# Two pads of 32 bytes ahead of the split activation tiles of a hybrid decoder block on one core

## The chip, the core and the metric

One core of one Trainium2 chip runs the whole program; the other seven are not used. The metric is the device time of one execution in microseconds (us), shown as the median of several runs. The engines are TensorE (PE for its matmuls, PEld for its weight loads), VectorE (DVE), ScalarE (ACT), GpSimd (POOL) and the queue of SyncE (SP), which issues the weight transfers.

## What is computed

The reference is one decoder block on 256 tokens of width 2048, in float32: a normed input projected to 14092 columns, four branches beside each other (a gated linear recurrence, a forgetting attention, a state space branch, an RWKV-7 branch), each gated and projected back, an output projection, a feed-forward part with a short convolution, and a gated addition at the end.

```python
def reference(x, p, ...):
    xn = rmsnorm(h, mix_norm[i])
    proj = jnp.einsum('bsd,dn->bsn', xn, w_in[i])
    ...
    gates = jax.nn.sigmoid(g_raw.astype(jnp.float32)).reshape(Bsz, S, N_BRANCH, D)
    for j in range(1, N_BRANCH):
        merged = merged + gates[:, :, j] * jnp.einsum('bsc,cd->bsd', branches[j], w_branch[i, j])
    h = h + jnp.einsum('bsd,de->bse', merged, w_out[i]).astype(h.dtype)
    hn = rmsnorm(h, ffn_norm[i])
    u = causal_dwconv(jnp.einsum('bsd,df->bsf', hn, w_up[i]), ffn_conv_w[i], ffn_conv_b[i])
    u_gate, u_val = jnp.split(u, 2, axis=-1)
    h = h + jnp.einsum('bsf,fd->bsd', jax.nn.gelu(u_gate) * u_val, w_down[i]).astype(h.dtype)
    pg = jax.nn.sigmoid(jnp.einsum('bsd,de->bse', rmsnorm(h, ple_norm[i]), w_ple_gate[i]))
    h = h + (pg * jnp.einsum('bsq,qd->bsd', p[i], w_ple[i])).astype(h.dtype)
    return h
```

## The kernel before

Every large product is made of weights that are streamed once from memory and activations that stay in SBUF, feature by token (128 features of a tile on the partitions, 256 tokens along each). Both are split into a high and a low part that the TensorE multiplies as float32r, so that one product becomes three: high by high, high by low, low by high.

**Weights.** `chunk` (lines 199 to 202) loads 512 KB into a tile `wr` (four buffers). `split` (204 to 210) lets ScalarE copy it to the high part `wh` (L208) and VectorE subtract that for the low part `wl` (L209), three buffers of 4096 bytes a partition each. A chunk holds four contraction steps k by two column blocks m.

**Activations.** `split_x` (226 to 230) puts the high part into the first 1024 bytes of a tile and the low part into the next 1024. Such tiles are `x` (pool `xp`, 16 buffers), `f` (the 44 tiles of the feed-forward part, pool `fp`), `p`, and for the output projection eight tiles `d` (pool `dp`) and eight quarters of tiles `e` (pool `bc`). `split_act` (220 to 224) makes two separate tiles instead, from pool `bp`, which the trace calls `sb`; the ys of the branches are of this kind.

**Products.** `product` (235 to 245) does one step of wide products in two matmuls: `wl` as stationary with the 256 columns of the high part, `wh` as stationary with all 512 columns of the tile. I call the two a pair; the wl matmul comes first except at k = 0. Where the activations come as two halves (the gates, from `xg`, line 1099, and the branch projections), lines 287 to 289 do three matmuls of 256 columns, with `wh`, `wh` and `wl`.

**Order.** `gemm_fm` (252 to 298) is one unit: for each chunk of four k it goes over m and k, then evacuates the PSUM banks. The units follow in program order: `w_ax`, 19 units of projections and `w_v` with the branches interleaved by `pump`, up to about 310 us; then gates (`gate_unit`, 1101) and branch projections (`branch_unit`, 1109) up to 840 us; `w_out` to 935; `w_up` (44 units, all with `x` tiles) to 1427; `w_down` (8 units of 44 k, with `f` tiles) to 1675; `w_ple_gate` (with `x`) to the end. The two priorities `g` and `m` and the order that the framework's list scheduler makes of them are the same in both kernels.

**Where tiles lie.** Pools are laid out in the order in which they are opened: `cst`, `wp`, `xp`, `sp`, then `bc`, `bp`, `dp`, and after these are closed `pp` and `fp` in their place. Tiles start at multiples of 32 bytes. In the built programs the start of a partition's bytes stands like this to 64:

| tile | what it is | first address before | beyond a multiple of 64, before | after |
|---|---|---|---|---|
| wh, wl | split weights, stationary | 36608, 48896 | 0 | 0 |
| x | split activations | 61184 | 0 | 32 |
| s | temporaries of 1024 bytes | 93952 | 0 | 32 |
| e | half of the activations of w_out | 119552 | 0 | 32 |
| p, f | split activations behind the branches | 119552, 123648 | 0 | 32 |
| sb | split ys of the branches, other temporaries | 175776 | 32 | 32 |
| d | the other half of the activations of w_out | 212640 | 32 | 32 |

Within a tile all the offsets that a wide matmul uses are multiples of 512 bytes, so the column holds for every matmul of the tile.

Of the kernel before, what the change touches and what calls it, by code (L numbers as in the profile page):

```python
# [7 lines left out]
F32 = mybir.dt.float32  # L8
# [6 lines left out]
P = 128  # L15
# [70 lines left out]
def body(tc, T, out, dbg=None):  # L86
    nc = tc.nc
    V, A, G, PE = nc.vector, nc.scalar, nc.gpsimd, nc.tensor
    ctx = ExitStack()
# [66 lines left out]

    cst = ctx.enter_context(tc.tile_pool(name="cst", bufs=1))
    wp = ctx.enter_context(tc.tile_pool(name="wp", bufs=2))
    xp = ctx.enter_context(tc.tile_pool(name="xp", bufs=16))
    sp = ctx.enter_context(tc.tile_pool(name="sp", bufs=25))  # L160
    psG = ctx.enter_context(tc.tile_pool(name="psG", bufs=4, space=bass.MemoryType.PSUM))
# [12 lines left out]
    bc_ = bctx.enter_context(tc.tile_pool(name="bc", bufs=1))  # L174
# [187 lines left out]
    act(junk, junk, AF.Identity)  # L362
    xraw, xs = [], []
    warm = bc_.tile([P, 512], F32, name="e", tag="e", bufs=3)
    V.memset(warm, 0.0)
    for k in range(KD // 2):
        xraw.append(dslot())
# [954 lines left out]
```

## Time and profile before

| | us |
|---|---|
| median of 3 runs (1774.45, 1783.17, 1775.72) | 1775.72 |
| the profiled execution's own time | 1783.29 |
| its span, first to last instruction | 1781.4 |
| TensorE busy in it | 1761.6 (99%) |
| VectorE, ScalarE, GpSimd busy | 1239.1, 942.8, 103.2 |

A busy share of TensorE close to 100% says only that matmuls overlap one another: the shown duration of one (some 390 ns for 512 columns) is longer than the time from one start to the next. What a matmul costs in a full stream is therefore read as a stretch of time divided by the matmuls that start in it. In the views by stretches the number behind x counts every instruction that lies in the stretch, so a stretch cut at the start of one matmul and of another counts one to three more than start in it.

### The profile page before, as it was taken

The page shows a single profiled execution, that of the slowest core. Times are in us where ns is not written, and L with a number is a line of the kernel's source. Part 1 is how long each engine was busy: PE and PEld are TensorE (multiplying, and loading weights), DVE is VectorE, ACT ScalarE, POOL GpSimd, SP SyncE. Part 2 cuts the span into 40 slices and gives each one's busy share as a digit, 9 for nine tenths or more (in the row PEclk, how much of TensorE's full clock was granted, in tenths as well). Part 3 has the DMA queues.
Part 4 walks back from the last instruction along what each step waited for, and adds up shares of the span by engine and source line. Part 5 has one row for each costly group of instructions (what it writes and reads, how often), then busy time and mean ns, then how long its engine had stood idle before and what let it go on. Part 6 is the DMA issues. An engine that isn't in the chain of part 4 may idle for free.

```text
span 1781.4 us, 29735 instructions
## 1 busy us (share of the span) xinstructions
PE 1761.6 (99%) x11621; PEld 1586.7 (89%) x11621; DVE 1239.1 (70%) x1998; ACT 942.8 (53%) x1422; POOL 103.2 (6%) x160
## 2 busy tenths in 40 slices
PE   8999999999999999999999999999999999999998
PEld 7887888999999999999888888888888888888887
DVE  8778667687789623567777777777777765555666
ACT  7577445556644423545556555555555544444554
POOL 4000000002310100000110000000000000000000
PEclk9999999999999979999999999999999999999999
DMA  8556556556665733555775555555556666665574
GB/s 278 172 169 193 166 171 211 185 173 204 204 211 177 246 107 113 171 179 180 232 229 188 188 188 184 186 187 189 186 184 195 210 204 191 191 190 185 171 227 131
DMA packets 98844, 336.27 MB, mean 189 GB/s; under 512 B 12330, under 2 KB 16592, under 8 KB 98704
## 3 DMA queue, kind: packets, MB, share of 16 engines
q1 hardware_dynamic: 90528, 310.94, 54.8%
q0 software_dynamic: 7456, 21.81, 4.2%
q8 instruction: 91, 1.49, 0.4%
q10 hardware_dynamic: 720, 1.63, 0.3%
q14 instruction: 49, 0.40, 0.1%
HBM read 324.85 MB, written 9.48 MB: 188 GB/s over the span
## 4 chain that ended last, share of the span: by engine, by line
PE 72%; issue 8%; DMA 1%; DVE 1%; POOL 0%; ACT 0%; POOLq 0%; DVEq 0%
PE pg L132 70%; PE pb L135 1%; PE pb L132 1%; DMA e<-fox_rn 0%; DVE wl L209 0%; DMA d<-rw_gn 0%; DMA rw_q<-e 0%; DMA rw_gn<-sb 0%; DVE s L100 0%; DVE e L888 0%; DVE sb L120 0%; POOL qbd L903 0%; POOL e L927 0%; DVE e L100 0%; POOL qat L899 0%
## 5 line engine op out<-in xcount | busy, mean ns | idle before, releaser
L132 PE MATMUL pg<-x,wh 128*128 128x512 f32 (+1 forms) x4384 | 1194.6, 346 | 2.4 <-DVE sb L100 2.4
L209 DVE TENSOR_TENSOR wl<-wr,wh 128x1024 fp32r<-128x1024 f32 (+1 forms) x592 | 717.3, 1213 | 433.1 <-ACT wh L208 425.3
L208 ACT CAST wh<-wr 128x1024 fp32r<-128x1024 f32 (+1 forms) x592 | 615.4, 1040 | 664.1 <-PE pg L132 519.7
L132 PE MATMUL pg<-x,wl 128*128 128x256 f32 (+1 forms) x3344 | 923.5, 284 | 10.1 <-DVE wl L209 10.1
L132 PEld LDWEIGHTS pg<-x,wh 128*128 128x128 f32 x4384 | 757.1, 190 | 100.8 <-issue 2.6
L132 PEld LDWEIGHTS pg<-x,wl 128*128 128x128 f32 (+1 forms) x3344 | 635.0, 190 | 24.9 <-DVE wl L209 12.9
L132 PE MATMUL pg<-f,wh 128*128 128x512 f32 x704 | 244.9, 395 | 0.0
L132 PE MATMUL pg<-f,wl 128*128 128x256 f32 x704 | 194.3, 280 | 0.0
L132 PEld LDWEIGHTS pg<-f,wh 128*128 128x128 f32 x704 | 131.6, 188 | 29.8
L132 PEld LDWEIGHTS pg<-f,wl 128*128 128x128 f32 x704 | 132.8, 189 | 1.1
L132 PE MATMUL pg<-sb,wh 128*128 128x256 f32 x512 | 95.5, 286 | 0.0
L120 DVE SCALAR_TENSOR_TENSOR s<-s,prm 128x255 f32<-128x255 f32 (+1 forms) x176 | 84.2, 478 | 1.7 <-ACT s L127 1.0
L132 PEld LDWEIGHTS pg<-sb,wh 128*128 128x128 f32 x512 | 80.6, 193 | 0.4
L249 ACT COPY s<-pg 128x256 f32<-128x256 f32 x136 | 49.6, 366 | 46.7 <-PE pg L132 46.2
L132 PE MATMUL pg<-sb,wl 128*128 128x256 f32 x256 | 73.2, 287 | 0.0
L100 DVE TENSOR_TENSOR s<-s 128x256 f32<-128x256 f32 (+1 forms) x172 | 70.7, 420 | 1.4
L100 DVE TENSOR_TENSOR s<-s,pg 128x256 f32<-128x256 f32 x136 | 56.3, 415 | 10.0 <-ACT s L249 8.3
L127 ACT ACTIVATE s<-s 128x256 f32<-128x256 f32 x140 | 56.4, 411 | 13.0 <-DVE s L100 12.7
L127 ACT ACTIVATE s<-s,prm 128x256 f32<-128x256 f32 x88 | 52.4, 595 | 0.7 <-DVE s L100 0.7
L127 ACT ACT_TABLE_LOAD x39 | 50.0, 1283 | 1.8 <-PEq L1312 1.2
L132 PEld LDWEIGHTS pg<-sb,wl 128*128 128x128 f32 x256 | 49.1, 192 | 0.5 <-issue 0.3
L132 PE MATMUL pg<-e,wh 128*128 128x512 f32 x128 | 45.6, 399 | 0.0
(232 smaller groups left out, 1211.2 us busy)
## 6 DMA issues: line engine op xcount, KB each, us to landing
wr<-in_w_up_dram SPq DMA_DIRECT2D x176, 512.0 KB, 3.6
wr<-in_w_g_dram SPq DMA_DIRECT2D x128, 512.0 KB, 3.7
wr<-in_w_down_dram SPq DMA_DIRECT2D x88, 512.0 KB, 4.2
wr<-in_w_p_dram SPq DMA_DIRECT2D x76, 512.0 KB, 3.9
wr<-in_w_branch_dram SPq DMA_DIRECT2D x32, 512.0 KB, 3.6
wr<-in_w_out_dram SPq DMA_DIRECT2D x32, 512.0 KB, 4.3
wr<-in_w_ple_gate_dram SPq DMA_DIRECT2D x32, 512.0 KB, 4.5
wr<-in_w_v_dram SPq DMA_DIRECT2D x8, 512.0 KB, 4.1
```

Source lines behind the costliest of these rows:

```text
L100: V.tensor_tensor(o, a, b, op=op)
L120: V.scalar_tensor_tensor(o, a, s, b, op0=op0, op1=op1)
L127: A.activation(o, i, f, **kw)
L132: return f(*a, **kw)
L135: f(*a, **kw)
L208: A.copy(wh, wr)
L209: V.tensor_tensor(wl, wr, wh.bitcast(F32), op=ALU.subtract)
L249: A.copy(o, pt[:, S:])
```

## The change

Before the pools `xp` and `sp` a pool with one tile of 32 bytes a partition is opened, so that all tiles behind it start 32 bytes later. In pool `bc`, behind the three `e` buffers, another tile of 32 bytes is allotted, so that the tiles behind it (the constants, `sb`, `d`) start 64 bytes later than before. Nothing reads or writes the pads. The lists of instructions of all engines, with their waits, sizes and buffers in turn, are the same in both kernels; only addresses differ: `x`, `s`, `e`, `p` and `f` by 32, what lies behind the second pad by 64, and `wr`, `wh`, `wl`, `prm2` and `R` by nothing.

```diff
     wp = ctx.enter_context(tc.tile_pool(name="wp", bufs=2))
+
+
+    pad = ctx.enter_context(tc.tile_pool(name="pad", bufs=1))
+    pad.tile([P, 8], F32, name="pad0")
     xp = ctx.enter_context(tc.tile_pool(name="xp", bufs=16))
...
     warm = bc_.tile([P, 512], F32, name="e", tag="e", bufs=3)
+    bc_.tile([P, 8], F32, name="pad1")
     V.memset(warm, 0.0)
```

## Rows read from the trace of the kernel before

**Rows 1.** The page's first part (busy us, share of the span, instructions of each engine), and the engines' shares of the chain of work that ended last.

```profile
PE 1761.6 (99%) x11621; PEld 1586.7 (89%) x11621; DVE 1239.1 (70%) x1998; ACT 942.8 (53%) x1422; POOL 103.2 (6%) x160
...
PE 72%; issue 8%; DMA 1%; DVE 1%; POOL 0%; ACT 0%; POOLq 0%; DVEq 0%
```

**Rows 2.** Who waited for whom over the whole span: engine, what it was to write, its line, whom it waited for; us in total, times, the longest.

```profile
ACT wh L208 <- PE pg L132: 519.7, 338, 4.2
...
DVE wl L209 <- ACT wh L208: 425.3, 352, 8.4
...
PE pg L132 <- DVE wl L209: 10.1, 7, 3.8
```

**Rows 3.** Stretches, TensorE alone: from and to, length, busy us and count, granted clock, share and rate of the DMA engines. The first is 360 gate matmuls on x, the second 160 of branch projections on sb, the third 400 pairs of w_up on x, the last three 80 pairs each of w_down on f, in its first, second and third unit.

```profile
770.11:813.31 43.20, 43.20 (x363) 1.00 0.60 190
820.59:839.36 18.77, 18.77 (x162) 1.00 0.55 179
1000.12:1141.29 141.17, 141.17 (x803) 1.00 0.59 187
1430.68:1458.94 28.26, 28.26 (x162) 1.00 0.66 205
1461.05:1488.78 27.73, 27.73 (x162) 1.00 0.63 196
1492.03:1519.76 27.73, 27.73 (x163) 1.00 0.62 191
```

**Rows 4.** Stretches in w_out, all engines: length, busy us and count of PE, PEld, DVE, ACT and POOL, granted clock, DMA share and rate. Each is eight pairs: the first and third on tiles d, the second and fourth on tiles e.

```profile
844.03:846.81 2.78, 2.78 (x17) 2.45 (x16) 2.78 (x6) 1.68 (x3) 0.00 (x0) 1.00 0.52 164
846.81:849.63 2.82, 2.82 (x17) 2.45 (x16) 2.12 (x4) 1.36 (x2) 0.00 (x0) 1.00 0.75 241
900.06:902.83 2.77, 2.77 (x17) 2.44 (x16) 2.60 (x6) 1.21 (x2) 0.61 (x2) 1.00 0.82 220
902.83:905.65 2.82, 2.82 (x17) 2.45 (x16) 1.22 (x1) 1.05 (x1) 0.00 (x0) 1.00 0.86 311
```

**Rows 5.** Groups of TensorE's matmuls by form in stretches 0 to 310 (first row), 310 to 600 (next two), 600 to 740 (two), 740 to 840 (two), 840 to 935, 935 to 1427, 1427 to 1675 and 1675 to the end (one each): count, then busy us and mean ns of one as modelled.

```profile
L132 PE MATMUL pg<-x,wh 128*128 128x512 f32 x640 | 226.0, 399 | 2.4 <-DVE sb L100 2.4
...
L132 PE MATMUL pg<-x,wh 128*128 128x256 f32 x1201 | 220.7, 284 | 0.0
L132 PE MATMUL pg<-x,wl 128*128 128x256 f32 x601 | 170.5, 286 | 0.0
...
L132 PE MATMUL pg<-x,wh 128*128 128x256 f32 x384 | 76.9, 296 | 0.0
L132 PE MATMUL pg<-x,wl 128*128 128x256 f32 x192 | 56.7, 295 | 0.0
...
L132 PE MATMUL pg<-x,wh 128*128 128x256 f32 x418 | 76.6, 287 | 0.0
L132 PE MATMUL pg<-x,wl 128*128 128x256 f32 x209 | 59.5, 286 | 1.9 <-DVE wl L209 1.9
...
L132 PE MATMUL pg<-e,wh 128*128 128x512 f32 x128 | 45.6, 399 | 0.0
...
L132 PE MATMUL pg<-x,wh 128*128 128x512 f32 x1395 | 486.3, 398 | 0.0
...
L132 PE MATMUL pg<-f,wh 128*128 128x512 f32 x704 | 244.9, 395 | 0.0
...
L132 PE MATMUL pg<-x,wh 128*128 128x512 f32 x253 | 89.5, 398 | 0.0
```

**Rows 6.** Stretches, all engines, columns as in rows 4: the gates and branch projections until 600, w_up, w_down.

```profile
310.00:600.00 290.00, 290.00 (x2406) 288.73 (x2405) 233.21 (x401) 156.95 (x235) 41.38 (x62) 1.00 0.63 196
...
935.00:1427.00 492.00, 492.00 (x2792) 427.51 (x2791) 374.29 (x610) 283.00 (x437) 5.92 (x11) 1.00 0.60 190
1427.00:1675.00 248.00, 248.00 (x1421) 216.85 (x1420) 134.74 (x162) 110.54 (x141) 3.76 (x7) 1.00 0.61 191
```

**Rows 7.** Groups of VectorE and ScalarE instructions by form: the same elementwise operation on tiles s and on tiles sb, and the copy to a high part on f and on sb (count, busy us, mean ns).

```profile
L100 DVE TENSOR_TENSOR s<-s 128x256 f32<-128x256 f32 x170 | 69.8, 420 | 1.4
...
L100 DVE TENSOR_TENSOR sb<-sb 128x256 f32<-128x256 f32 x34 | 13.9, 421 | 5.1 <-ACT sb L127 4.8
...
L214 ACT CAST f<-s 128x256 fp32r<-128x256 f32 x44 | 17.4, 394 | 0.0
...
L214 ACT CAST sb<-sb 128x256 fp32r<-128x256 f32 x38 | 14.7, 403 | 15.4 <-DVE sb L100 11.9 <-DVE sb L120 3.1
```

**Rows 8.** Stretches of ten us about the narrow matmuls of the RWKV branch, columns as in rows 4; the granted clock is the third number from the end.

```profile
620.00:630.00 10.00, 10.00 (x108) 9.71 (x106) 1.65 (x2) 2.81 (x5) 0.00 (x0) 0.73 0.21 71
630.00:640.00 10.00, 10.00 (x51) 8.12 (x49) 2.50 (x4) 2.54 (x6) 0.00 (x0) 0.50 0.16 54
640.00:650.00 10.00, 10.00 (x66) 9.18 (x67) 2.10 (x4) 2.81 (x4) 0.00 (x0) 0.58 0.17 52
...
760.00:770.00 10.00, 10.00 (x73) 10.00 (x73) 10.00 (x21) 5.36 (x10) 0.00 (x0) 0.83 0.62 177
```

**Rows 9.** The timeline of TensorE inside w_up: start in us, duration in us, engine, line, operation, output and operands.

```profile
1103.63 0.40 PE L132 MATMUL pg<-x,wh 128*128 128x512 f32 x1
1103.87 0.28 PE L132 MATMUL pg<-x,wl 128*128 128x256 f32 x1
1103.99 0.40 PE L132 MATMUL pg<-x,wh 128*128 128x512 f32 x1
```

## The prediction

> **What bounds the kernel now.** I read the shares first, then the waits, then the pitch of the matmuls. TensorE is busy 99% of the span, and 72% of the chain that ended last is its own work [rows 1]. The waits say the same from the other side: the longest total is ScalarE waiting 519.7 us for TensorE to give back a buffer `wh`, VectorE waits 425.3 us behind ScalarE, while TensorE waited for VectorE's low parts 10.1 us in all [rows 2]. So the weights are ready ahead of time nearly everywhere, and time goes from one matmul's start to the next. What the change can touch is this pitch, and only where a stretch holds matmuls back to back.
>
> The pitch is not the same everywhere. In w_up, on tiles `x`, 400 pairs took 141.17 us, 352.9 ns a pair. In w_down, on tiles `f`, 80 pairs took 28.26 us in the first unit (353.3 ns a pair) and 27.73 us in the second and third (346.6) [rows 3]. All at full granted clock, with the DMA engines at about the same load. In w_out one and the same unit goes over tiles `d` and then over tiles `e`, with the same weights buffers, sizes and order: eight pairs on `d` took 2.78 and 2.77 us (346.9 ns a pair), eight on `e` 2.82 twice (352.5) [rows 4]. With 256 columns throughout, 360 gate matmuls on `x` took 43.20 us, 120.0 ns each, and 160 of a branch projection on `sb` 18.77 us, 117.3 ns each [rows 3].
>
> Set beside the table of addresses, `d` and `sb` start 32 bytes beyond a multiple of 64 and are quick, `x` and `e` start on one and are slow, `f` starts on one and is either. That is an experiment that the kernel already holds: the change puts `x`, `e`, `f` and `p` where `d` and `sb` stand. `f` tells something more. Its two speeds go by whole units at unchanged addresses, so an offset of 0 does not force the slow pitch; it allows a slow rhythm that a unit falls into at its start and stays in. In no stretch on `d` or `sb` that I looked at does that rhythm appear.
>
> **The change part by part.** No instruction is added, removed or moved, and no wait. The pads cost no time. What may change is (a) the matmul pitch, (b) the time that other engines need for tiles at other addresses, (c) phases against the clock.
>
> (a) *Wide pairs.* The quick price is that of `d`, 346.9; the slow one 352.5 (e) to 352.9 (x, with the starts of units in it). I take 5.7 ns a pair, between the 5.6 of `e` against `d` and the 6.0 of `x` against `d`. The counts are in [rows 5]:
> w_up, 1395 pairs: 8.0 us. Half of w_out, 128 pairs on `e`: 0.7. The last stage, 253 pairs on `x`: 1.4, and 0.1 for the 32 on `p`. w_down: 248.0 us hold 1421 matmuls [rows 6], 13 more than the 704 pairs on `f`; less these 2.3 us it is 349.0 ns a pair, 2.1 above `d`: 1.5. The projections before 310 us, 640 pairs: here weights come late at times and units are mixed with narrow matmuls; from nothing (all already quick or hidden by other waits) to 3.6 us (640 by 5.7); I take the middle, 2.0, because no row gives it.
>
> *Matmuls of 256 columns.* On `x` there are 1201, 601, 384, 192, 418 and 209, in all 3005 [rows 5]. At 120.0 less 117.3 ns they give 8.1 us. Not all run at 120.0: about 100 lie where the clock is halved [rows 8], and those behind a change from `sb` may start quick. I take 7.0; the lower bound is about half, 4, should the branch's own work on VectorE, busy 233 of 290 us from 310 to 600 [rows 6], pace this stage in part. Against this stands that TensorE had no idle time there at all, 290.00 busy of 290.00, and only 1.9 us behind `wl` later [rows 5, 6].
>
> Sum: 8.0 + 0.7 + 1.4 + 0.1 + 1.5 + 2.0 + 7.0 = 20.7 us. What covers for the faster TensorE: it must be fed 1.6 to 2.3% sooner. In w_up VectorE is busy 374 of 492 us and the DMA engines 60% [rows 6], so nobody comes near to taking the bound over. ScalarE's wait for a buffer gets shorter by what TensorE gains, and becomes the reserve that is used up: 519.7 us of it against 20.7.
>
> (b) *Other engines.* The same elementwise operation takes VectorE 420 ns on `s` and 421 on `sb`, and ScalarE's copy to a high part 394 on `f` and 403 on `sb` [rows 7]. With `s` moved to the offset of `sb` I cost this at nothing; even 9 ns on all of ScalarE's copies would lie under its waits. The upper bound is some 1 us, at the ends of units, where an evacuation is awaited.
>
> (c) *Clock.* Around 620 to 650 us, behind a run of narrow matmuls of the RWKV branch, the granted clock is 0.73, 0.50 and 0.58 in three stretches of ten us, and 0.83 once more at 760 [rows 8]. At half clock the time is twice that at full: 2.7 + 5.0 + 4.2 + 1.7 = 13.6 us are lost there. TensorE will come there earlier, by perhaps 5 us, and how long the clock stays at 1.2 GHz can come out otherwise, by all of this downward and by about as much upward. I take no change.
>
> The profiled execution took 1783.29 us, so the sum for it is 1762.6. The median of the runs shown is 7.6 us below it, and one of the three runs, 1783.17, lies where the profiled one does. The saving is a sum over matmuls that every run makes, so I take it off the median: 1775.7 less 20.7 is **1755.0 us**.
>
> **The rivals.**
>
> *The offset does nothing.* `d` and `sb` also lie highest in SBUF, and the two rhythms of `f` show that starts of units matter. If the starts decide alone, w_up may stay as it is and units of `f` may change sides: the mean of 349.0 between 346.6 and 353.3 makes five in eight quick, and these to slow would cost 440 by 6.7 ns, 2.9 us. The result is 1774 to 1779. Against it: tiles `f` spread over the same addresses as `sb` and are slow in whole units; and the turn from `d` to `e` comes inside a unit, twice alike [rows 4]. This is also what the Trainium skill would have: "TensorE: Matmul & The Clock Gate", section "Step-by-step: what each phase is for", says that the array has two separate read ports to SBUF, so that loading the next weights takes nothing from the matmul that runs. By it, where the two operands lie to each other could not matter, and the time would stay at 1775.7. The trace does not agree as it stands: 2.78 against 2.82 us for the same eight pairs. Chance 0.12.
>
> *It locks in a worse place (slower).* `d` and `sb` stand 160 bytes beyond a multiple of 256, `x` and `f` will stand 32 beyond one. If a longer period than 64 bytes counts, the new place may hold a rhythm slower than 352.9 ns; from there on it is a loss. Within the slow rhythm single pairs are longer than its mean: from one wide matmul's start to the next 0.36 us [rows 9], some 361 ns. If all wide pairs took that: 8.1 ns by about 1776 pairs on `x` and `e` of w_up, w_out and the last stage are 14.4 us, 12.0 by 704 on `f` 8.4: 1798.5. Nothing in the trace shows a stretch at that mean. Chance 0.04.
>
> *It works in part.* The wide pairs follow `d`, the gates don't follow `sb`, since `sb` holds its two halves in separate tiles and `xg` in one: 13.7 us, 1762. The other way round, 9 us: 1766.7. Chance 0.16, most of it still faster by over 0.5%.
>
> **How the numbers follow.** The forecast has 0.68, the partial case 0.16, no effect 0.12, the worse rhythm 0.04. Changes under 0.5% (8.9 us) are about what a measurement of this kernel can't tell from none, so the mark for faster is 1766.8. Faster: 0.68 and 0.13 of the partial case, 0.81; same: 0.12 and 0.03, 0.15; slower 0.04. The range goes down to 1746: the lowest run, 1774.45, less the upper ends of the terms (1395 by 6.0 is 8.4, then 0.8, 1.5, 0.1, 1.6, 3.6, 8.1; 24.1 in all) is 1750, and a part of the clock's 13.6 us below that. It goes up to 1770: the partial case at 1766.7 and a part of the clock's loss. That leaves out no effect and the worse rhythm.
>
> **What would show it.** Right: w_up from its first to its last unit in about 484 us in place of 492; 80 pairs of w_down near 27.75 us in every unit, none at 28.26; `e` like `d` in w_out; gate matmuls at 117.3 ns; TensorE's waits as small as before. Wrong: w_up still at 352.9 ns a pair (no effect), or over it (a worse rhythm); gates at 120.0 (partial); pitches as forecast, but waits for `wl` of more than 5 us above the 10.1 (someone else becomes the bound); or all this right and the stretches at half clock longer by 15 us or more.

## The result and the profile after

The changed kernel takes 1755.67 us, the median of 4 runs (1752.78 to 1759.45); the kernel before, beside it, 1776.98 (1774.45 to 1783.17). The ratio is 0.9884, with a 95% interval of 0.9856 to 0.9913. Timed a second time, six runs against eleven, the ratio was 0.9907 (0.9877 to 0.9937). The profiled execution took 1754.74 us, with a span of 1752.9.

The same instructions as in [rows 3], now in the changed kernel (from and to, length, busy us and count, granted clock, DMA share and rate): 360 gate matmuls on x, 160 of a branch projection on sb, 400 pairs of w_up, 80 pairs each of w_down's first three units.

```profile
753.85:795.85 42.00, 42.00 (x363) 1.00 0.62 202
802.98:821.91 18.93, 18.93 (x162) 1.00 0.57 181
981.31:1120.23 138.92, 138.92 (x803) 1.00 0.60 190
1405.02:1432.75 27.73, 27.73 (x162) 1.00 0.68 211
1434.84:1462.58 27.74, 27.74 (x161) 1.00 0.62 198
1465.84:1493.57 27.73, 27.73 (x162) 1.00 0.61 190
```

The gates went from 120.0 to 116.7 ns a matmul, w_up from 352.9 to 347.3 ns a pair, and w_down's slow unit is gone: all three shown take 27.73 or 27.74 us. The matmuls on sb, which the second pad moved by 64 bytes, became slower, from 117.3 to 118.3 ns. The eight pairs on d and e of [rows 4], same view:

```profile
826.61:829.44 2.83, 2.83 (x18) 1.00 0.53 122
829.44:832.22 2.78, 2.78 (x18) 1.00 0.76 237
882.36:885.14 2.78, 2.78 (x18) 1.00 0.71 200
885.14:887.92 2.78, 2.78 (x17) 1.00 0.91 332
```

The tiles e (second and fourth row) fell from 2.82 to 2.78 us. The tiles d, also moved by 64, are slow in one stretch (2.83 for 2.78) and as quick as before in the other (2.78 for 2.77). The whole of w_up, against the row of [rows 6], all engines (PE, PEld, DVE, ACT, POOL):

```profile
919.90:1404.00 484.10, 484.10 (x2790) 427.67 (x2789) 374.52 (x610) 283.17 (x438) 5.92 (x11) 1.00 0.61 193
```

484.10 us in place of 492.00, with VectorE and ScalarE busy for as long as before: nobody else became the bound. The waits of TensorE for low parts are 10.5 us in all against 10.1, but they are longer in the projections (first 312 us). In the changed kernel:

```profile
PE pg L132 <- DVE wl L213: 10.0, 7, 3.8
```

and in the kernel before:

```profile
PE pg L132 <- DVE wl L209: 8.2, 6, 3.8
```

Of the 1.8 us more, 1.2 lie in the first 20 us, where e1 (below), with the pitches of the kernel before, waits as long. The first 20 us of the kernel before, of the changed one and of e1:

```profile
PE pg L132 <- DVE wl L209: 0.7, 2, 0.4
...
PE pg L132 <- DVE wl L213: 1.9, 2, 1.4
...
PE pg L132 <- DVE wl L211: 1.8, 2, 1.5
```

One difference can't be put down to the change, as its repeat below shows. The stretches about the narrow matmuls, as in [rows 8], in the profiled execution of the changed kernel.

```profile
620.00:630.00 10.00, 10.00 (x124) 9.08 (x123) 3.64 (x6) 3.90 (x8) 0.00 (x0) 1.00 0.20 57
630.00:640.00 10.00, 10.00 (x97) 9.04 (x98) 3.71 (x5) 3.23 (x5) 0.00 (x0) 1.00 0.32 104
640.00:650.00 10.00, 10.00 (x119) 9.80 (x118) 3.21 (x5) 2.59 (x4) 0.75 (x1) 1.00 0.62 210
```

The granted clock is 1.00 here, where it was 0.73, 0.50 and 0.58. So the two profiled executions differ by 28.6 us, of which about 12 are the clock's: the mean over the span is 0.997 against 0.990. To compare kernels apart from it I take from each run's time its span times one less its mean clock, and call this *less the clock*. It is an estimate. It is somewhat too large, since it takes the lower clock for half the speed, and gate matmuls at 0.50 took 213.4 ns and not twice their 120.0 (rows in the last section); and the clocks are recorded to 0.001, which leaves 0.9 us either way in each run.

### The profile page after: what moved, and what is told of

Read it like the earlier page. It is cut to its first block, busy times and chain, and to the rows that moved or that the text cites. A ratio compares the mean times of both kernels' runs of the same rounds, so it can differ in the third digit from the quotient of the medians.

```text
span 1752.9 us, 29735 instructions
## 1 busy us (share of the span) xinstructions
PE 1731.9 (99%) x11621; PEld 1572.4 (90%) x11621; DVE 1238.4 (71%) x1998; ACT 943.1 (54%) x1422; POOL 103.2 (6%) x160
## 4 chain that ended last, share of the span: by engine, by line
PE 73%; issue 8%; DMA 1%; DVE 1%; POOL 0%; ACT 0%; POOLq 0%; DVEq 0%
PE pg L132 71%; PE pb L135 1%; PE pb L132 1%; DMA rw_q<-e 0%; DMA e<-fox_rn 0%; DMA d<-rw_gn 0%; DVE wl L213 0%; DVE sb L120 0%; DVE s L100 0%; DMA rw_gn<-sb 0%; POOL qbd L908 0%; POOL e L932 0%; DVE sb L100 0%; POOL qat L904 0%; DVE e L893 0%
## 5 line engine op out<-in xcount | busy, mean ns | idle before, releaser
L132 PE MATMUL pg<-x,wh 128*128 128x512 f32 (+1 forms) x4384 | 1170.7, 339 | 3.0 <-DVE sb L100 2.4
L132 PE MATMUL pg<-x,wl 128*128 128x256 f32 (+1 forms) x3344 | 919.6, 283 | 10.6 <-DVE wl L213 10.5
L132 PEld LDWEIGHTS pg<-x,wh 128*128 128x128 f32 x4384 | 746.3, 188 | 89.7 <-issue 3.6
```

The source lines that it names most:

```text
L132: return f(*a, **kw)
```

## The experiments

All twelve kernels have the same instructions, waits and buffers on every engine as the kernel before; only addresses differ, so each is given by its pads. All but the last are shown as edits of the kernel before; e2 is the changed kernel with one more pad. Two theories at first: **A**, the distance between the moving tile and the stationary weights sets the pitch; **B**, the moving tile's own place does (32 bytes beyond a multiple of 64 is quick). The rival that the region of SBUF or the starts of units decide is tested along with them. In the profiles below each row is one of the stretches shown above, found by its instructions.

**e1: everything moved by 32.**

```diff
+    padw = ctx.enter_context(tc.tile_pool(name="padw", bufs=1))
+    padw.tile([P, 8], F32, name="padw0")
     wp = ctx.enter_context(tc.tile_pool(name="wp", bufs=2))
```

> One pad of 32 bytes ahead of the weights pool, none elsewhere: weights and activations x, s, e, f, p all at 32 beyond a multiple of 64, sb and d on a multiple, so every distance between two operands is as in the kernel before. Theory A (the distance between the stationary and the moving operand sets the rhythm): nothing changes, ratio 0.998 to 1.002, w_up at 352.9 ns a pair, gate matmuls on x at 120.0 ns, d still quick at 347. Theory B (the moving operand's own place counts, 32 beyond a multiple of 64 is quick): as the changed kernel for x, e and f, slow for d and sb, ratio about 0.990, w_up at 347.3 ns a pair.

Ratio 0.9998 (0.9977 to 1.0019). The gates and w_up:

```profile
770.26:813.46 43.20, 43.20 (x362) 1.00 0.63 196
...
1000.32:1141.50 141.18, 141.18 (x803) 1.00 0.61 187
```

To 0.01 us the kernel before. The x tiles stand at 32 here, as in the changed kernel, and are slow: theory B falls.

**e2: weights at 32, activations on multiples of 64.** To the changed kernel everything from the weights on lies 32 bytes later, so that every distance is the changed kernel's.

```diff
+    padw = ctx.enter_context(tc.tile_pool(name="padw", bufs=1))
+    padw.tile([P, 8], F32, name="padw0")
     wp = ctx.enter_context(tc.tile_pool(name="wp", bufs=2))
+    pad = ctx.enter_context(tc.tile_pool(name="pad", bufs=1))
+    pad.tile([P, 8], F32, name="pad0")
     xp = ctx.enter_context(tc.tile_pool(name="xp", bufs=16))
...
+    bc_.tile([P, 8], F32, name="pad1")
```

> Weights at 32 beyond a multiple of 64, all activations (x, s, e, f, p, sb, d) on a multiple: the changed kernel's distance with the places swapped. Theory A (distance): ratio 0.986 to 0.990, w_up near 347.3 ns a pair, gate matmuls below 118 ns. Theory B (the moving operand's own place): no gain, ratio 1.000 to 1.003, w_up at 352.9 ns, d and sb slow as well.

```profile
758.21:800.21 42.00, 42.00 (x362) 1.00 0.64 198
807.35:826.28 18.93, 18.93 (x162) 1.00 0.62 184
985.68:1124.59 138.91, 138.91 (x802) 1.00 0.61 189
```

The pitches are those of the changed kernel, as theory A has it. The ratio, 0.9920 (0.9891 to 0.9949), missed what was expected: three of its four runs had a mean clock of 0.991 or 0.992, while all four of the changed kernel's had 0.996 to 0.998. Less the clock the medians are 1750.8 (e2), 1751.0 (changed), 1767.3 (e1) and 1767.7 (before, 19 runs).

**e3: the first pad of the change alone.**

```diff
+    pad = ctx.enter_context(tc.tile_pool(name="pad", bufs=1))
+    pad.tile([P, 8], F32, name="pad0")
     xp = ctx.enter_context(tc.tile_pool(name="xp", bufs=16))
```

> The first pad alone: x, s, e, f, p at 32, but what lies behind e shifts by 32, so that sb and d come onto a multiple of 64 like the weights. Theories A and B both: x, e and f quick as in the changed kernel, d at 352 to 353 ns a pair and sb at 120 ns, which gives back 128 by 5.5 ns and 768 by 2 ns, 2.2 us: ratio 0.988 to 0.992. If the region of SBUF and not the place to 64 makes d and sb quick, they stay at 347 and 117.

```profile
803.79:822.63 18.84, 18.84 (x162) 1.00 0.58 182
982.38:1121.30 138.92, 138.92 (x803) 1.00 0.62 190
...
827.33:830.15 2.82, 2.82 (x17) 1.00 0.51 163
...
883.27:886.09 2.82, 2.82 (x17) 1.00 0.76 240
```

w_up as in the changed kernel. The d pairs became slow as expected, but sb did not: 117.8 ns here at a multiple of 64, where x had 120.0. Ratio 0.9913 (0.9879 to 0.9947), less the clock 1748.4: the second pad brings nothing that these runs can show. A period of 64 no longer explains sb.

**e4: the first pad with 64 bytes.** The edit of e3 with `[P, 16]`.

> The first pad with 64 bytes in place of 32, no second: x, s, e, f, p on a multiple of 64 again, but 64 beyond one of 256 and not on it; sb and d exactly where the changed kernel has them. If only the distance to 64 counts: slow, ratio 0.998 to 1.004, w_up at 352.9 ns a pair, gates on x at 120.0. If a longer period counts: w_up at another pitch than both 352.9 and 347.3.

```profile
764.61:807.01 42.40, 42.40 (x363) 1.00 0.65 200
...
994.15:1135.20 141.05, 141.05 (x802) 1.00 0.60 187
1424.33:1452.60 28.27, 28.27 (x162) 1.00 0.70 207
1454.69:1482.95 28.26, 28.26 (x161) 1.00 0.60 191
```

Ratio 0.9994 (0.9973 to 1.0015): slow again, w_up at 352.6. Yet it isn't the kernel before: gates at 117.8 in place of 120.0, and w_down's second unit slow too, which had been quick. The period is longer than 64; the gates show it, since w_down's units had two speeds at one and the same place already.

**e5, e6 and e7: 96, 128 and 192 bytes.** The same edit with `[P, 24]`, `[P, 32]` and `[P, 48]`, one run each.

> The first pad with 96 bytes, no second: x, s, e, f, p 96 beyond a multiple of 512 from the weights, sb and d at distance 0, where x was before. Period of 64: x, e, f at 347 ns a pair and gates on x at 117 ns, as in the changed kernel; sb at 120.0 ns and d at 352.5 to 353. If the region of SBUF makes sb and d quick, they stay at 117 and 347. Longer period: x at another pitch than 347.3 and 116.9.

> The first pad with 128 bytes, no second: x, e, f, p at a distance of 128 from the weights, sb and d at 32, where the changed kernel has x. Period of 64 or 128: w_up at 352 to 353 ns a pair, gates on x at 120.0 ns; sb at 116.9 ns, d at 347.3. Period of 256 or 512: w_up or the gates at another pitch.

> The first pad with 192 bytes, no second: x, e, f, p at a distance of 192, sb and d at 96. Period of 64: w_up at 353 ns a pair, gates on x at 120.0 ns. Period of 256: x behaves as sb and d did at 448 in the kernel with the first pad alone, gates at 115.5 ns and w_up near 352. sb and d at 96: as x in the kernel with 96 bytes.

Times of 1773.81, 1773.49 and 1767.57 us beside 1773.98 for the kernel before. The gates on x, the branch projection on sb, and w_up, of e5:

```profile
763.29:806.49 43.20, 43.20 (x362) 1.00 0.58 190
813.80:833.00 19.20, 19.20 (x162) 1.00 0.58 180
993.47:1133.64 140.17, 140.17 (x803) 1.00 0.60 188
```

of e6:

```profile
762.99:805.71 42.72, 42.72 (x362) 1.00 0.62 198
812.92:831.59 18.67, 18.67 (x163) 1.00 0.56 179
991.83:1132.20 140.37, 140.37 (x802) 1.00 0.60 188
```

and of e7:

```profile
753.02:793.82 40.80, 40.80 (x362) 1.00 0.67 203
800.82:820.02 19.20, 19.20 (x162) 1.00 0.61 182
981.62:1122.79 141.17, 141.17 (x802) 1.00 0.58 187
```

sb at distance 0 (e5) takes 120.0 ns, what x took there; at 32 (e6) 116.7, what x takes in the changed kernel; at 96 (e7) 120.0, as x in e5. The region of SBUF falls: the tiles sb follow the distance. At 96, an odd multiple of 32, x is slow in the gates and halfway in w_up (350.4), and at 192 the gates take 113.3 in this stretch, the quickest of all, with w_up at 352.9. Wide pairs and matmuls of 256 columns don't like the same distance.

One stretch isn't the whole kernel, though. Earlier in e7, 96 gate matmuls on x at the same distance took 117.8 ns each (first row), which is what sb takes at 192 in e3. The second row is from g, the changed kernel's repeat: 96 gate matmuls at 117.8, where the long stretch of that kernel has 116.7.

```profile
547.80:559.11 11.31, 11.31 (x98) 1.00 0.49 149
...
592.51:603.82 11.31, 11.31 (x99) 1.00 1.03 335
```

**e8: wh and wl at different distances.** As e3, but the pad lies between wh and wl, so that x is at 32 from wh and 0 from wl.

```diff
     wp = ctx.enter_context(tc.tile_pool(name="wp", bufs=2))
+    padl = ctx.enter_context(tc.tile_pool(name="padl", bufs=1))
+    padl.tile([P, 8], F32, name="padl0")
+    wlp = ctx.enter_context(tc.tile_pool(name="wlp", bufs=2))
...
-        wl = wp.tile([P, kn, cols], F32R, name="wl", tag="wl", bufs=3)
+        wl = wlp.tile([P, kn, cols], F32R, name="wl", tag="wl", bufs=3)
```

> The kernel with the first pad alone, but with the pad between wh and wl: x, e, f, p and wl at 32, wh on a multiple of 64, so that the moving tile is at distance 32 from wh and 0 from wl. If what counts is the moving tile against the weights that are loaded while it streams, the wide matmul (wl is loaded under it) goes back to the slow one's 236 ns and the narrow one (wh is loaded under it) stays at 118, some 352 to 354 ns a pair; gates between 117 and 120. If the matmul's own stationary tile counts, the wide one (wh) stays at 229 and the narrow one (wl) gets slower, 120. If the two matter only together: a pitch outside both.

One run, 1748.24 us:

```profile
752.95:795.08 42.13, 42.13 (x363) 1.00 0.61 201
...
980.32:1118.15 137.83, 137.83 (x802) 1.00 0.61 191
```

344.6 ns a pair, below anything before. By the starts of the 400 pairs the gain on e3 is in the wide matmul, 226.7 ns to the next start for 229.1 (the narrow one 117.9 for 118.2); the change's own gain was there too, 229.1 for 235.8 (narrow: 118.2 for 117.1). The theory that a matmul is held up by the weights that load while it streams falls: wl, at distance 0, loads under the wide matmul, and the pair got shorter, not longer. That the matmul's own stationary tile counts fits no better: nothing got slower either. What is left of the three readings is the last, that the two distances matter together.

**f2 and f3: two more pairs of distances.** The edit of e8 with the pad between wh and wl at 224 bytes and the first pad at 32 (f2: x at 0 from wh, 32 from wl), or at 32 and 160 bytes (f3: x at 192 from wh, 160 from wl); one run each.

> wl moved the other way: x at 0 from wh as before the change and at 32 from wl (to 256), sb and d at 160 from wh as before. If the wide matmul's pitch is set by the place of wl, which is loaded while it streams: 229 or below in w_up and the narrow one near 117, 345 to 348 ns a pair. If the moving tile's distance to wh sets it: 352 to 354. Gates on x: two of three loads are of wh, so near 120 if wh counts, below 118 if wl does.

> x at 192 from wh, where the gates were quickest (115.0 ns), with wl moved by 32, so at 160 from wl. If the step of 32 between wh and wl is what made pairs quick whatever the distance of x: 344 to 347 ns a pair in w_up and gates still near 115. If each distance counts by itself: pairs between 347.5 (160) and 352.9 (192). If only the one combination of 32 and 0 is quick: 352 or more.

1771.31 and 1784.31 us, at mean clocks of 0.998 and 0.992. The gates and w_up of f2:

```profile
756.16:798.56 42.40, 42.40 (x362) 1.00 0.61 200
...
986.05:1127.05 141.00, 141.00 (x803) 1.00 0.57 187
```

and of f3:

```profile
767.60:810.39 42.79, 42.79 (x362) 1.00 0.61 197
...
997.88:1139.13 141.25, 141.25 (x802) 1.00 0.59 186
```

Neither is quick, 352.5 and 353.1. Neither wl's distance of 32 alone nor the step between wh and wl makes a pair quick. In w_up f2 went as it would if the distance to wh alone counted, in the gates (117.8) as if wl did; and e8 against e3, at the same 32 to wh, differs by 2.7 ns, so wl counts too.

**f1: e8 with sb and d brought to the same distances.** The edit of e8 and a pad `[P, 24]` where the change has its second. **g: the changed kernel again**, beside it on the same chip; its edit is the change.

> As the kernel with the pad between wh and wl (x at 32 from wh, 0 from wl), and 96 bytes more behind the tiles e, so that sb and d lie at 32 and 0 too (to 256). If the pitch depends only on the moving tile's distances to wh and wl, to 256: w_up 344.7 ns a pair, d the same (352.6 before this step, 1.0 us), sb 117.5 as the gates on x (118.4, 0.7 us); 1.7 us off that kernel, some 6 to 8 us off the changed kernel at the same clock, ratio to the kernel before 0.982 to 0.987.

> The changed kernel once more, beside the one before. If the pitch gives 16.7 us and the rest of the first comparison (21.3 us) was a more favourable clock in its runs: less the time that the clock took, 16 to 17 us off the kernel before; the median anywhere from 1753 to 1764, by how many runs have a mean clock of 0.991 and how many 0.997. If the whole 21 us are the change's: a median of 1754 to 1757 and a higher mean clock than the kernel before in nearly every run.

f1 took 1748.94 us (1747.99 to 1751.97, 5 runs), ratio 0.9833 (0.9806 to 0.9861): quicker than both kernels, at mean clocks of 0.997 to 0.999. g took 1763.38 (1755.32 to 1768.11, 6 runs), the kernel before 1780.71 (11 runs). Of f1, the branch projection on sb, w_up and the two stretches on d:

```profile
804.10:822.83 18.73, 18.73 (x163) 1.00 0.55 182
981.61:1119.44 137.83, 137.83 (x802) 1.00 0.59 191
...
827.48:830.23 2.75, 2.75 (x17) 1.00 0.43 127
...
882.85:885.60 2.75, 2.75 (x17) 1.00 0.78 231
```

d fell from 2.82 and 2.83 us in e8 to 2.75, sb from 118.9 to 117.1 ns, as expected. The whole time fell short of what was expected: less the clock 4.6 us off g in place of 6 to 8, and no better than e8's one run (1744.7). g settles the clock: two of its six runs had 0.997 (1755.32 and 1756.63), four 0.990 to 0.992 (1762.31 to 1768.11). Less the clock: before 1766.8, g 1750.0, f1 1745.4. The change's own part is 16.8 us in this comparison, and 16.7 when its first four runs are set against the 19 of the kernel before beside e1 to e4.

All together, with distances to 256, one long stretch for each figure. That distances repeat at 256 rests on few cells: sb in e8 and x in f3 are alike to 256 and not to 512, and both take 118.9 ns.

| kernel | x to wh, wl | w_up, ns a pair | gates on x, ns | sb to wh, wl | sb, ns |
|---|---|---|---|---|---|
| before, e1 | 0, 0 | 352.9 | 120.0 | 160, 160 | 117.3 |
| changed, e2 | 32, 32 | 347.3 | 116.7 | 224, 224 | 118.3 |
| e3 | 32, 32 | 347.3 | 116.7 | 192, 192 | 117.8 |
| e4 | 64, 64 | 352.6 | 117.8 | 224, 224 | 118.3 |
| e5 | 96, 96 | 350.4 | 120.0 | 0, 0 | 120.0 |
| e6 | 128, 128 | 350.9 | 118.7 | 32, 32 | 116.7 |
| e7 | 192, 192 | 352.9 | 113.3 | 96, 96 | 120.0 |
| e8 | 32, 0 | 344.6 | 117.0 | 192, 160 | 118.9 |
| f1 | 32, 0 | 344.6 | 117.0 | 32, 0 | 117.1 |
| f2 | 0, 32 | 352.5 | 117.8 | 160, 192 | 118.8 |
| f3 | 192, 160 | 353.1 | 118.9 | 96, 64 | 117.8 |

## Why the prediction was right, and where its sizes were off

**The mechanism** was right in its core, and that is now shown: where the tiles lie sets the pitch, through the distance of the moving tile to the weights. e1 leaves every distance and changes nothing, though x then stands 32 bytes beyond a multiple of 64; e2 has the changed kernel's distances at other places, and its pitches; sb has the pitches of x at the same distances in another region. The rule that the forecast drew, 32 beyond a multiple of 64, was wrong twice: the moving tile's own place doesn't count (the weights stood at 0, so that the kernel before couldn't tell), and 64 isn't the period. "No effect" falls.

A clash of TensorE with another engine's accesses is no rival. In w_up of the kernel before a pair took 353.5 ns where VectorE was idle throughout it (54 pairs) and 353.6 where it was busy throughout (217); 354.9 and 354.4 with ScalarE idle (106) and busy (138); 353.6 and 353.8 with fewer and more DMA transfers under way than in the median pair. The rule of separate read ports in the Trainium skill, "TensorE: Matmul & The Clock Gate", section "Step-by-step: what each phase is for", does not agree with these runs as far as time goes: by it the distance should not matter, and e1 and e2, whose weights lie at the same place and whose x lie 32 bytes apart, take 141.18 and 138.91 us for the same 400 pairs. What the two reads do to each other inside the chip no run shows.

**Term by term**, less the clock, between the two profiled executions at the same instruction: w_up gave 7.7 us (forecast 8.0), w_down 1.7 (1.5), w_out 0.5 (0.7), the last stage 1.3 (1.5 with p). The projections gave nothing, -0.2 for a forecast of 2.0, which was the lower bound given. The longer wait of the first 20 us isn't the change's, since e1 has it too; from 38 us to their end the same instructions gained 0.2 us, and why not more stays open. The gates and branches gave 5.7 for 7.0 (in g 4.5); the gates on x gained more than forecast (3.3 ns in the stretch for 2.7), the matmuls on sb lost 1.0 ns by their 64 bytes. The latter step was missing: I took sb and d for untouched because their place to 64 was unchanged. In sum 16.6 us for 20.7. Set against the kernel before in the same way, e1, whose pitches are unchanged, comes out at -1.9, all of it in the projections and the gates, so these two terms are good to about 2 us. Two slips in the forecast matter little: 32 pairs on p at 5.7 ns are 0.2 us and not 0.1, and the partial case "the other way round" has 9 us where the sum's own term for 256 columns is 7.0.

**The clock** made the forecast look better than it was. It was taken as unchanged, and its loss was reckoned too high (13.6 us, as if half the clock took twice the time; gate matmuls took 1.78 times). In the first comparison the changed kernel's four runs happened to have a mean of 0.996 to 0.998, which added about 4.6 of the 21.3 us. With g's six runs the difference of medians is 17.3 us. Runs of one and the same kernel differ by some 10 us with the mean clock alone, more than the half per cent that the chances were worked out for.

**The rival of a longer period** was right in its doubt and wrong in its outcome: the pitch does repeat only beyond 64 bytes (e4's gates against before's; e5 at 96 has 120.0 and 350.4 where 32 has 116.7 and 347.3), so d and sb at 160 were no proof for x at 32. That 32 was about as good as 160 was luck; 64 bytes of padding would have brought nothing (e4), nor would 96 (e5). By their single profiled executions, set against the kernel before as above, 128 brought some 3 us (e6) and 192 some 5 (e7), with those 2 us of doubt.

**Open**: why these distances, and why one distance can hold two rhythms. Neither the distance to wh nor that to wl explains the pairs alone, and the wide pairs and the matmuls of 256 columns rank the distances differently. Which reads meet, the runs don't tell.

## What to carry to other kernels

When TensorE is the bound and its pitch is over what the same matmul takes elsewhere in the kernel, group its start-to-start times by the addresses of the two operands before anything else: tiles of two pools in one unit are an experiment that is already in the trace. Try the pads by measurement, wh and wl apart, since no simple rule held; 32 bytes between the two weights tiles, with 96 behind the tiles e, gave more than the change (f1: 1745.4 against 1750.0 us less the clock). Compare such small gains at the same granted clock, or by the length of the same run of instructions in two traces.

## What the runs showed of the hardware

Matmuls in a full stream at full granted clock fall into steady rhythms, repeated to 0.01 us over 400 pairs in other kernels with the same distances: 137.83 us in e8 and f1, 138.91 or 138.92 in the changed kernel, e2 and e3, 141.17 or 141.18 in before and e1. Moving all tiles alike changes nothing.

One distance can hold two rhythms, and w_down's units keep the one that they start in. At distance 0 its first unit took 28.26 us and the next two 27.73 [rows 3]; at 192 the gates of e7 took 117.8 and later 113.3 ns a matmul. At 32 all the w_down units shown are quick, but the gates have 116.7 and, in a stretch of g, 117.8.

At half the granted clock the distance made no difference. Of the gate matmuls on x, 14 of the kernel before (distance 0, first row) took 213.4 ns each by their starts, 13 of e7 (distance 192, second row) 213.3, where they take 120.0 and 113.3 in the long stretches at full clock.

```profile
761.28:764.27 2.99, 2.99 (x16) 0.50 0.46 138
...
744.14:746.91 2.77, 2.77 (x15) 0.50 0.49 180
```

Runs of one kernel have different mean granted clocks, 0.990 to 0.998 in the 11 of the kernel before beside g, and with them times that differ by some 10 us. In the profiled executions with 0.990 to 0.993 (before, e1, e4, f3) most of the low clock lies behind the narrow matmuls of the RWKV branch, between 620 and 650 us; in that of the changed kernel these stretches have 1.00.
